# Splitting the first w_out pieces between the merge blocks, and the last output tile in two column halves

## The chip, the cores and the metric

The kernel runs on one core of a Trainium2 chip. The metric is the device time of one execution in microseconds (us); less is better. The core's engines work side by side, each through its own queue of instructions in the order of that queue: TensorE (PE) multiplies into PSUM banks; VectorE (DVE) and ScalarE (ACT) do elementwise work; SyncE (SP) issues most transfers between DRAM and the core's memory (DMA); GpSimd (POOL) does little here. An instruction waits on semaphores for its inputs and for the buffers that it writes.

## The reference

One encoder block on x of 1024 x 1024 in float32. Two mixers, a multi-scale pooling path and a chunked gated linear attention (GLA), are merged by sigmoid gates and projected by w_out; a squared-ReLU MLP and a last norm follow.

```python
def hybrid_mixer(u, w_in, ...):
    z = jnp.einsum('bld,dn->bln', u, w_in)
    a, q, k, v, r, lr, ga, gb = jnp.split(z, IN_SPLITS, axis=-1)
...
    y_a = jnp.einsum('blc,cd->bld', p, w_pool_out)
...
    y_b = jnp.einsum('blc,cd->bld', o.reshape(B, L, GLA_VAL), w_gla_out)
    m = jax.nn.sigmoid(ga) * y_a + jax.nn.sigmoid(gb) * y_b
    return jnp.einsum('bld,de->ble', m, w_out)

def squared_relu_mlp(u, w_ff1, w_ff2):
    hdn = jnp.square(jax.nn.relu(jnp.einsum('bld,df->blf', u, w_ff1)))
    return jnp.einsum('blf,fd->bld', hdn, w_ff2)

def reference(x, meta_tokens, norm_mix, ...):
...
        h = h + hybrid_mixer(rmsnorm(h, norm_mix[l]), ...)
        h = h + squared_relu_mlp(rmsnorm(h, norm_ffn[l]), w_ff1[l], w_ff2[l])
    return rmsnorm(h, norm_final)[:, N_META:]
```

## The kernel before, in words

Every float32 product is made of three matmuls (the helper mm3, lines L280, L281, L282): each operand is split into a high part and a low part, and high x high, high x low and low x high are added in one PSUM bank of 128 x 512. So a weight, once it is loaded, has to be split before PE can use it: ACT copies it to the high part, and DVE subtracts that from the weight for the low part. Bank names in the trace begin with b_: b_mm is a rotating tag, b_oa the last layer's.

The program is written as steps (`step(rest, ...)`) that are recorded in the order of the code and then placed in the engines' queues by a scheduler; an instruction given to `keep_in_program_order` stays where the code has it. Each engine works its queue strictly from front to back, so an instruction that waits holds up everything behind it on its engine.

**The merge stage** (about 479 to 512 us). For the second half of the rows, `yb(j)` (L1316) computes two groups of the merge, d = 2j and 2j + 1, in `yb_block` (L1072): 12 matmuls of the GLA output (tile yg) with w_gla_out into a b_mm bank. The weights of j = 2 and 3 are kept in their split form from before; those of 0 and 1 are loaded again (tile raw) and split into w1h and w1l on ACT L84 and DVE L85, 128 x 1024 at a time. Behind a group DVE multiplies the bank with the gate (L1095, tiles o and t: this frees the bank; the gate gb comes from DRAM by an SP DMA of L1037), adds the other mixer's part (L1096, ma from DRAM), ACT makes the high half th (L1099), and DVE the low half tl (L1100). The projection `out_tile(t, ch)` (L1262) then multiplies a row tile t of the merged result, half by half of the columns ch, with w_out: 24 matmuls, and a DVE add (L1277). `x_again` loads x once more for that add.

w_out's first half arrives in four pieces of 256 rows, kk = 0 to 3, each 128 x 1024 in the core: `load_wo(0, kk)` issues the DMA (L1243), and splits it on ACT (L1244) and DVE (L1245) into the tile wo. Piece kk holds the blocks 2kk and 2kk + 1 of the eight that one out tile adds up, so piece 3 is used by an out tile's last six matmuls. The steps stand in this order: yb(2), the four load_wo, yb(3), yb(0), x_again for rows 0 and 1, out_tile(0, 0), yb(1), out_tile(1, 0), and then the other six.

**The tail** (from about 1209 us). The last of the MLP's second layer's products (`m == 6`) are added for four row tiles, t = 0 to 3, each in a bank b_oa of its own: nine matmuls per row from three late pairs (`product`). Then, row by row: DVE adds the bank to the residual (L1536), `finish_row` squares half a row on ACT with a sum (L1512), computes the inverse root in small steps (L232 to L240), scales half h1 on ACT (L1515) and half h0 on DVE (L1516), and SP issues both output DMAs (L1518).

Of the kernel before, what the change touches and what calls it, by code (L numbers as in the profile page):

```python
# [10 lines left out]
ACT = mybir.ActivationFunctionType  # L11
ALU = mybir.AluOpType
AX = mybir.AxisListType

P = 128
D = 1024
# [3 lines left out]
HALF = 512  # L20
# [9 lines left out]
NPAIR = DFF // P // 2  # L30
# [92 lines left out]
def kernel(  # L123
# [60 lines left out]
    gB = left.push("gB", [P, D], F32)  # L184
# [16 lines left out]
    raw = Raw(nc, [left.push(f"raw{i}", [P, D], F32) for i in range(2)])  # L201
# [10 lines left out]
    def f32(ap):  # L212
        return ap.bitcast(F32)
# [4 lines left out]
    def bcast(v):  # L218
        return v[None, :].broadcast_to([P, D])
# [56 lines left out]
    def mm3(ps, n, lhs, rhs, first=True, last=True, more=False):  # L276

        for i in range(n):
            (ah, al), (bh, bl) = lhs(i), rhs(i)
            pe.matmul(ps, ah, bh, start=first and i == 0, stop=False, skip_group_check=more)  # L280
            pe.matmul(ps, ah, bl, start=False, stop=False, skip_group_check=more)  # L281
            pe.matmul(ps, al, bh, start=False, stop=last and i == n - 1, skip_group_check=more)  # L282
# [83 lines left out]
    def halves():  # L366
        return [slice(h * HALF, (h + 1) * HALF) for h in range(2)]
# [541 lines left out]
    decs = tiny(4 * NC)  # L909
# [75 lines left out]
    rest, fill, done = [], [], set()  # L985
# [80 lines left out]
    def rows4(w, j):  # L1066
        return w[:, j * 256 : (j + 1) * 256].rearrange("(k p) c -> p k c", p=P)
# [143 lines left out]
    MERGE = (2, 3, 0, 1)  # L1211
# [18 lines left out]
    def x_again(*rows):  # L1230
        for t in rows:
            tc.keep_in_program_order(nc.sync.dma_start(S["acc"][:, t], x[t * P : (t + 1) * P, :]))

    def load_wo(ch, kk):
        def fn():
            wo = S["wo"][ch][:, :, 2 * kk : 2 * kk + 2]
            c = slice(ch * HALF, (ch + 1) * HALF)
            src = w_out[kk * 256 : (kk + 1) * 256, c].rearrange("(k p) c -> p k c", p=P)
            if ch:
                r = raw.load(src, D).rearrange("p (k c) -> p k c", k=2)  # L1240
            else:
                r = S["acc"][:, 4 + kk].rearrange("p (k c) -> p k c", k=2)
                nc.sync.dma_start(r, src)  # L1243
            act.activation(wo[:, 0], r, ACT.Copy)  # L1244
            dve.tensor_tensor(wo[:, 1], r, f32(wo[:, 0]), ALU.subtract)  # L1245

        return fn

    step(rest, merge_open)
    def wo1_open():  # L1250
# [77 lines left out]
    step(rest, wo1_open)  # L1328
    for t in range(2, 8):
# [170 lines left out]
    def finish_row(t, tail):  # L1500

        a, (h0, h1) = S["c"][:, t], halves()
        junk = S["w2"]["12"].rearrange("p i c -> p (i c)")[:, (t % 4) * D : (t % 4 + 1) * D]
        if not tail:
            ss = ln_stat[t % 4]
            act.activation(junk, a, ACT.Square, accum_out=ss)
            rs = inv_sqrt(ss, 1, 1.0 / D)
            dve.scalar_tensor_tensor(junk, a, rs, gB, ALU.mult, ALU.mult)
            nc.sync.dma_start(out[t * P : (t + 1) * P, :], junk)
            return  # L1510
        s0, s1 = tails[t]
        act.activation(junk[:, h0], a[:, h0], ACT.Square, accum_out=s0)  # L1512
        dve.tensor_scalar(s1, s1, 1.0 / D, EPS, ALU.mult, ALU.add)
        rs = inv_sqrt(s0, 1, 1.0 / D, s1)
        act.activation(junk[:, h1], a[:, h1], ACT.Copy, scale=rs)  # L1515
        dve.scalar_tensor_tensor(junk[:, h0], a[:, h0], rs, gB[:, h0], ALU.mult, ALU.mult)  # L1516
        for c in (h1, h0):
            nc.sync.dma_start(out[t * P : (t + 1) * P, c], junk[:, c])  # L1518

    tails = [(decs[:, 2 * i : 2 * i + 1], decs[:, 2 * i + 1 : 2 * i + 2]) for i in range(4)]  # L1520

    def ff2():
        nc.sync.dma_start(gB, bcast(norm_final))
        h1 = halves()[1]
        b, late = None, []

        def product(t, i, av, bv):
            (ah, al), (bh, bl) = av, bv
            c = slice(t * P, (t + 1) * P)
            mm3(b[t], 1, lambda _: (ah[:, c], al[:, c]), lambda _: (bh, bl), first=i == 0, last=i == NPAIR - 1)  # L1530

        def leave(m, t, b):
            for r, k, sign in FF2[m][2]:
                a = S["c"][:, 4 * r + t, k * HALF : (k + 1) * HALF]
                if sign > 0:
                    dve.tensor_tensor(a, b[t], a, ALU.add)  # L1536
                else:
                    dve.tensor_tensor(a, a, b[t], ALU.subtract)

        def left_over(m, t, b):  # L1540
            leave(m, t, b)
            if m == 4:
                yield
                finish_row(4 + t, False)
            elif m == 5:
                yield
                a = S["c"][:, t, h1]
                junk = S["w2"]["12"][:, 8 + t]
                act.activation(junk, a, ACT.Square, accum_out=tails[t][1])
                dve.tensor_tensor(a, a, gB[:, h1], ALU.mult)  # L1550
            yield

        def left_overs(m, b):
            for t in range(4):
                yield from left_over(m, t, b)

        todo = iter(())
        for m, i, av, bv in ahead(ff2_operands(), 2):
            if i == 0:
                b = [bank("ob" if m % 2 else "oa") for _ in range(4)]  # L1560
            if m == 6 and i >= NPAIR - 3:
                late.append((i, av, bv))
            else:
                for t in range(4):
                    product(t, i, av, bv)
# [12 lines left out]
    def ff_layers():  # L1578

# [57 lines left out]
```

## Time and profile before

| | |
|---|---|
| median of 3 runs | 1222.71 us (1220.06 to 1222.97) |
| the profiled execution | 1222.77 us, of it 1221.0 us span |
| starts of the last matmul ahead of d7 and of the first of out_tile(1, 0) | 491.04 to 511.76 us |
| longest PE wait in the merge stage | 1.17 us, at 492.59, ended by DVE L1095 |
| PE's last matmul starts | 1212.89 us |
| last output DMA is issued | 1217.6 us |

Times in the trace are counted from the start of the span. A row of the timeline has start, duration, engine, line, operation, output<-input, shapes, and in brackets the idle time of the engine ahead of it and what ended it. SPq is SP's queue of DMA issues; PEld is PE's loading of weights, which runs beside its matmuls. d0 to d7 name the eight groups of the merge; they run in the order 4, 5, 6, 7, 0, 1, 2, 3.

### The profile page before, as it was taken

How to read it: one execution, taken by the hardware profiler on the slowest of the kernel's cores; microseconds unless marked ns; L12 is line 12 of the kernel's file. 1: busy time of each engine (PE TensorE's matmuls, PEld its weight loads, DVE VectorE, ACT ScalarE, POOL GpSimd, SP SyncE). 2: the span in 40 equal slices, each digit the busy share in tenths (PEclk: the TensorE clock that was granted, in tenths of full speed). 3: DMA queues.
4: the chain of work that ended last, by engine and by line, in shares of the span. 5: the costliest groups of instructions: out<-in, count | busy, mean ns of one | idle time of the engine just before them, and what ended most of it. 6: DMA issues, size and time to landing. Idle time of an engine off the chain costs nothing.

```text
span 1221.0 us, 18366 instructions
## 1 busy us (share of the span) xinstructions
PE 1207.9 (99%) x6807; PEld 997.2 (82%) x6807; DVE 838.9 (69%) x1381; ACT 572.0 (47%) x1009; POOL 75.5 (6%) x96
## 2 busy tenths in 40 slices
PE   9999999999999999999999999999999999999997
PEld 6998977778778888788778888888888888888886
DVE  6535657665777569825887677676775887887686
ACT  7627444444456224314655455454554444444544
POOL 0000043222330000000000000000000000000000
PEclk9999999999999999999999999999999999999999
DMA  8313334435247977921244444444569973333532
GB/s 236 93 40 95 118 100 130 147 105 164 81 137 266 318 243 233 323 67 69 104 139 156 141 163 151 150 155 145 172 228 326 332 246 104 96 95 96 171 95 88
DMA packets 153356, 192.76 MB, mean 158 GB/s; under 512 B 12178, under 2 KB 88226, under 8 KB 153267
## 3 DMA queue, kind: packets, MB, share of 16 engines
q1 hardware_dynamic: 153266, 191.59, 48.9%
q8 instruction: 53, 0.87, 0.3%
q14 instruction: 37, 0.30, 0.1%
HBM read 128.62 MB, written 62.93 MB: 157 GB/s over the span
## 4 chain that ended last, share of the span: by engine, by line
PE 89%; DVE 4%; DMA 2%; ACT 2%; issue 2%; POOL 0%; SPq 0%; POOLq 0%; ACTq 0%; DVEq 0%
PE b_mm L280 7%; PE b_mm L282 7%; PE b_mm L281 7%; PE b_y L280 6%; PE b_y L282 6%; PE b_y L281 6%; PE b_oa L282 5%; PE b_oa L281 5%; PE b_oa L280 5%; PE b_z L280 4%; PE b_z L282 4%; PE b_z L281 4%; PE b_sc L280 4%; PE b_ob L281 4%; PE b_ob L282 4%; PE b_ob L280 4%
## 5 line engine op out<-in xcount | busy, mean ns | idle before, releaser
L685 ACT ACTIVATE w1h<-raw 128x512 fp32r<-128x512 f32 x106 | 65.9, 622 | 59.3 <-PE b_y L281 25.3
L686 DVE TENSOR_TENSOR w1l<-raw,w1h 128x512 fp32r<-128x512 f32 x106 | 72.4, 684 | 22.0 <-ACT w1h L685 22.0
L280 PE MATMUL b_sc<-th,w1h 128*128 128x512 f32 x216 | 85.6, 396 | 0.6 <-ACT u2p L1420 0.6
L280 PE MATMUL b_z<-th,w1h 128*128 128x512 f32 x216 | 85.3, 395 | 0.5 <-DVE c L804 0.3
L281 PE MATMUL b_sc<-tl,w1h 128*128 128x512 f32 x216 | 84.9, 393 | 0.0
L281 PE MATMUL b_z<-tl,w1h 128*128 128x512 f32 x216 | 84.3, 390 | 0.4 <-DVE tl L1306 0.4
L282 PE MATMUL b_sc<-th,w1l 128*128 128x512 f32 x216 | 84.4, 391 | 0.0
L685 ACT ACTIVATE w1h<-fs 128x512 fp32r<-128x512 f32 x81 | 51.1, 631 | 70.7 <-PE b_y L281 32.9
L282 PE MATMUL b_z<-th,w1l 128*128 128x512 f32 x216 | 84.1, 389 | 0.0
L686 DVE TENSOR_TENSOR w1l<-fs,w1h 128x512 fp32r<-128x512 f32 x81 | 57.1, 705 | 26.1 <-ACT w1h L685 25.9
L280 PE MATMUL b_mm<-th,w1h 128*128 128x512 f32 (+1 forms) x208 | 72.1, 347 | 0.0
L281 PE MATMUL b_mm<-tl,w1h 128*128 128x512 f32 (+1 forms) x208 | 71.0, 341 | 0.0
L282 PE MATMUL b_mm<-th,w1l 128*128 128x512 f32 (+1 forms) x208 | 71.0, 341 | 0.0
L685 ACT ACTIVATE w1h<-bt 128x512 fp32r<-128x512 f32 x46 | 29.1, 632 | 70.9 <-issue 43.9
L1496 DVE TENSOR_TENSOR bt<-w,w 128x512 f32<-128x512 f32 x80 | 54.6, 683 | 1.0 <-DMA w<-in_w_ff_dram 0.9
L280 PE MATMUL b_mm<-wo,th 128*128 128x512 f32 x128 | 50.4, 393 | 0.0
L282 PE MATMUL b_mm<-wo,tl 128*128 128x512 f32 x128 | 49.9, 390 | 0.0
L281 PE MATMUL b_mm<-wo,th 128*128 128x512 f32 x128 | 49.8, 389 | 0.0
L280 PE MATMUL b_y<-wo,w1h 128*128 128x512 f32 x128 | 49.8, 389 | 0.0
L281 PE MATMUL b_y<-wo,w1h 128*128 128x512 f32 x128 | 49.8, 389 | 0.0
L282 PE MATMUL b_y<-wo,w1l 128*128 128x512 f32 x128 | 49.8, 389 | 0.0
L686 DVE TENSOR_TENSOR w1l<-bt,w1h 128x512 fp32r<-128x512 f32 x46 | 31.7, 690 | 25.6 <-ACT w1h L685 25.6
(405 smaller groups left out, 3334.6 us busy)
## 6 DMA issues: line engine op xcount, KB each, us to landing
hf_dram<-h SPq DMA_DIRECT2D x112, 256.0 KB, 2.1
raw<-hf_dram SPq DMA_DIRECT2D x112, 256.0 KB, 2.6
w<-in_w_ff_dram SPq DMA_DIRECT2D x64, 256.0 KB, 4.5
raw<-in_w_in_dram SPq DMA_DIRECT2D x22, 512.0 KB, 4.3
raw<-in_w_ff_dram SPq DMA_DIRECT2D x16, 512.0 KB, 4.2
rawx<-in_w_ff_dram SPq DMA_DIRECT2D x16, 512.0 KB, 4.2
rawp<-in_w_in_dram SPq DMA_DIRECT2D x10, 512.0 KB, 4.4
xs<-in_x_dram SPq DMA_DIRECT2D x8, 512.0 KB, 4.8
```

The source lines that it names most:

```text
L280: pe.matmul(ps, ah, bh, start=first and i == 0, stop=False, skip_group_check=more)
L281: pe.matmul(ps, ah, bl, start=False, stop=False, skip_group_check=more)
L282: pe.matmul(ps, al, bh, start=False, stop=last and i == n - 1, skip_group_check=more)
L685: act.activation(hi, a, ACT.Copy)
L686: dve.tensor_tensor(lo, a, f32(hi), ALU.subtract)
L1496: dve.tensor_tensor(bt, w, S["w2"][q[3:]][:, i], ALU.add if q[2] == "+" else ALU.subtract)
```

## The change

Two things are rewritten. In the merge stage, all four DMAs of w_out's first half are issued ahead of yb(2) (`fetch_wo`), one piece is split behind each of the four yb blocks (`first_wo`, its two instructions kept in program order), and the out tiles (0, 0) and (1, 0) stand behind all four blocks. In the tail, row 3 is computed by `last_tile` in two column halves of 256: nine matmuls, an add and a square with sum each, the two sums joined by a small add; row 2's scaling and output are put behind row 3's sums; and row 3's two output DMAs are issued by two queues, h1 by ACT's and h0 by SP's.

```diff
+    def split_wo(ch, kk, r):
+        wo = S["wo"][ch][:, :, 2 * kk : 2 * kk + 2]
+        a = act.activation(wo[:, 0], r, ACT.Copy)
+        return a, dve.tensor_tensor(wo[:, 1], r, f32(wo[:, 0]), ALU.subtract)
+
+    def fetch_wo():
+        for kk in range(4):
+            nc.sync.dma_start(wo_place(kk), wo_source(0, kk))
+
+    def first_wo(kk):
+        for ins in split_wo(0, kk, wo_place(kk)):
+            tc.keep_in_program_order(ins)
...
-    yb(2)
-    for k in range(4):
-        step(rest, load_wo(0, k))
-    yb(3)
-    yb(0)
+    step(rest, fetch_wo)
+    for k, j in enumerate(MERGE):
+        yb(j)
+        step(rest, lambda k=k: first_wo(k))
     step(rest, lambda: x_again(0, 1))
     step(rest, out_tile(0, 0))
-    yb(1)
     step(rest, out_tile(1, 0))
...
+        def put():
+            o = act.activation(junk[:, h1], a[:, h1], ACT.Copy, scale=rs)
+            if t > 1:
+                tc.keep_in_program_order(o)
+            (nc.scalar if t == 3 else nc.sync).dma_start(out[t * P : (t + 1) * P, h1], junk[:, h1])
+            dve.scalar_tensor_tensor(junk[:, h0], a[:, h0], rs, gB[:, h0], ALU.mult, ALU.mult)
+            nc.sync.dma_start(out[t * P : (t + 1) * P, h0], junk[:, h0])
+
+        return put
+
+    def last_tile(t, late, product, b, put):
...
+        for q, ss in ((0, decs[:, 8:9]), (1, s0)):
+            c = slice(q * 256, (q + 1) * 256)
+            for x in late:
+                product(t, *x, c)
+            dve.tensor_tensor(a[:, c], b[t][:, c], a[:, c], ALU.add)
+            act.activation(junk[:, c], a[:, c], ACT.Square, accum_out=ss)
+            if q == 0:
+                dve.tensor_tensor(s1, s1, ss, ALU.add)
+        last = finish_tail(t, s0, s1)
+        put()
+        last()
...
-            for t in range(4):
+            for t in range(3):
                 for x in late:
                     product(t, *x)
                 leave(m, t, b)
-                finish_row(t, True)
+                if t < 2:
+                    finish_row(t, True)
+            a, (s0, s1) = S["c"][:, 2], tails[2]
+            act.activation(S["w2"]["12"][:, 4], a[:, : HALF], ACT.Square, accum_out=s0)
+            last_tile(3, late, product, b, finish_tail(2, s0, s1))
```

MERGE is (2, 3, 0, 1). The new lines for what moved: the split is L1242 on ACT and L1243 on DVE, the out tile's add L1284, the half add L1545, the half square L1546, the scalings L1528 and L1532.

First place: DVE's queue in the merge stage, from the last low half of the first half of the rows. Before:

```order
L1245 TENSOR_TENSOR wo0_4699<-acc_4703,wo0_4699 128x1024 [waits DMAHW5_49,Activation_49]
L1100 SCALAR_TENSOR_TENSOR tl0_140<-o_3841,th0_136 128x512 [waits Activation_49]
L1245 TENSOR_TENSOR wo0_4699<-acc_4703,wo0_4699 128x1024 [waits DMAHW6_49,Activation_49]
L1245 TENSOR_TENSOR wo0_4699<-acc_4703,wo0_4699 128x1024 [waits DMAHW7_49,Activation_49]
L85 TENSOR_TENSOR w1l_132<-raw0_120,w1h_128 128x1024 [waits DMAHW1_49,PE_49,Activation_49]
L1095 SCALAR_TENSOR_TENSOR o_4715<-o_4715,b_mm_4780 128x512 [waits DMAHW0_49,PE_49]
L1095 SCALAR_TENSOR_TENSOR t1_4711<-t1_4711,b_mm_4727 128x512 [waits DMAHW5_49,DVE_49]
```

and in the changed kernel, from the same low half (its second row before, its first row now):

```order
L1100 SCALAR_TENSOR_TENSOR tl0_140<-o_3841,th0_136 128x512 [waits Activation_49]
L85 TENSOR_TENSOR w1l_132<-raw0_120,w1h_128 128x1024 [waits DMAHW1_49,PE_49,Activation_49]
L1095 SCALAR_TENSOR_TENSOR t1_4711<-t1_4711,b_mm_4731 128x512 [waits DMAHW3_49,DVE_49]
L1095 SCALAR_TENSOR_TENSOR o_4715<-o_4715,b_mm_4774 128x512 [waits DMAHW0_49,PE_49]
L1096 TENSOR_TENSOR t1_4711<-t1_4711 128x512 [waits DMAHW4_49,DVE_49]
L1095 SCALAR_TENSOR_TENSOR t1_4711<-t1_4711,b_mm_4750 128x512 [waits DMAHW5_49]
L1096 TENSOR_TENSOR o_4715<-o_4715 128x512 [waits DMAHW1_49,DVE_49]
L1100 SCALAR_TENSOR_TENSOR tl1_148<-t1_4711,th1_144 128x512 [waits Activation_49]
```

Three splits of w_out have left the place between that low half and the first merge instructions. The last of the four now stands here, behind the low half of the last group (d3, whose bank is b_mm_4871):

```order
L1243 TENSOR_TENSOR wo0_4699<-acc_4703,wo0_4699 128x1024 [waits Activation_49]
L1100 SCALAR_TENSOR_TENSOR tl1_148<-o_4715,th1_144 128x512 [waits Activation_49]
L1095 SCALAR_TENSOR_TENSOR o_4715<-o_4715,b_mm_4871 128x512 [waits DMAHW3_49,PE_49]
L1096 TENSOR_TENSOR o_4715<-o_4715 128x512 [waits DMAHW1_49,DVE_49]
L1100 SCALAR_TENSOR_TENSOR tl1_148<-o_4715,th1_144 128x512 [waits Activation_49]
L1243 TENSOR_TENSOR wo0_4699<-acc_4703,wo0_4699 128x1024 [waits Activation_49]
```

From the first merge instruction L1095 to this last split, 28 rows stand on DVE: L85 once, L1243 three times, and 24 rows of 128x512.

Second place: PE's queue in out_tile(0, 0), from its 13th matmul to its 21st. Before, where yb(1) still stands behind it:

```order
L280 MATMUL b_mm_4859<-wo0_4699,th0_136 128x512
L281 MATMUL b_mm_4859<-wo0_4699,th0_136 128x512
L282 MATMUL b_mm_4859<-wo0_4699,tl0_140 128x512
L280 MATMUL b_mm_4859<-wo0_4699,th0_136 128x512
L281 MATMUL b_mm_4859<-wo0_4699,th0_136 128x512
L282 MATMUL b_mm_4859<-wo0_4699,tl0_140 128x512
L280 MATMUL b_mm_4859<-wo0_4699,th0_136 128x512 [waits Activation_49]
L281 MATMUL b_mm_4859<-wo0_4699,th0_136 128x512
```

and now, behind yb(1):

```order
L280 MATMUL b_mm_4893<-wo0_4699,th0_136 128x512 [waits Activation_49]
L281 MATMUL b_mm_4893<-wo0_4699,th0_136 128x512 [waits DVE_49]
L282 MATMUL b_mm_4893<-wo0_4699,tl0_140 128x512
L280 MATMUL b_mm_4893<-wo0_4699,th0_136 128x512
L281 MATMUL b_mm_4893<-wo0_4699,th0_136 128x512
L282 MATMUL b_mm_4893<-wo0_4699,tl0_140 128x512
L280 MATMUL b_mm_4893<-wo0_4699,th0_136 128x512 [waits Activation_49]
L281 MATMUL b_mm_4893<-wo0_4699,th0_136 128x512 [waits DVE_49]
```

Each of the pieces 2, 3 and 4 (kk = 1, 2, 3) is now waited for where it is first used, its high half by L280 for ACT and its low half by L281 for DVE; the rows shown are those of the third and the fourth piece.

Third place: PE's last matmuls, row 3 of the tail, where the first column half ends and the second begins. Before, the row's nine matmuls are 512 wide and none of them waits. Now:

```order
L280 MATMUL b_oa_9704<-w1h_128 128x256
L281 MATMUL b_oa_9704<-w1l_132,w1h_128 128x256
L282 MATMUL b_oa_9704<-w1h_128,w1l_132 128x256
L280 MATMUL b_oa_9704<-fxh_7802,w1h_128 128x256 [waits DVE_49]
L281 MATMUL b_oa_9704<-fxl_7806,w1h_128 128x256
```

The first matmul of the second half carries a wait for DVE; both halves write the same bank, b_oa_9704.

More of the change, by code (lines that the diff above doesn't have):

```diff
@@ L1232, in x_again, with wo_source, wo_place @@
             tc.keep_in_program_order(nc.sync.dma_start(S["acc"][:, t], x[t * P : (t + 1) * P, :]))
-    def load_wo(ch, kk):
[L1235 to L1247, printed above, removed]
+    def wo_source(ch, kk):
+        return w_out[kk * 256 : (kk + 1) * 256, ch * HALF : (ch + 1) * HALF].rearrange("(k p) c -> p k c", p=P)
+    def wo_place(kk):
+        return S["acc"][:, 4 + kk].rearrange("p (k c) -> p k c", k=2)
+    def split_wo(ch, kk, r):
[8 more added lines that the diff above has]
+            tc.keep_in_program_order(ins)
+    def load_wo(ch, kk):
+        return lambda: split_wo(ch, kk, raw.load(wo_source(ch, kk), D).rearrange("p (k c) -> p k c", k=2)) and None
     step(rest, merge_open)
@@ L1512, in finish_row, with finish_tail @@
         act.activation(junk[:, h0], a[:, h0], ACT.Square, accum_out=s0)
+        finish_tail(t, s0, s1)()
+    def finish_tail(t, s0, s1):
+        a, (h0, h1) = S["c"][:, t], halves()
+        junk = S["w2"]["12"].rearrange("p i c -> p (i c)")[:, t * D : (t + 1) * D]
         dve.tensor_scalar(s1, s1, 1.0 / D, EPS, ALU.mult, ALU.add)
         rs = inv_sqrt(s0, 1, 1.0 / D, s1)
[L1515 to L1518, printed above, removed]
+        def put():
[7 more added lines that the diff above has]
+    def last_tile(t, late, product, b, put):
+        a, (s0, s1) = S["c"][:, t], tails[t]
+        junk = S["w2"]["12"].rearrange("p i c -> p (i c)")[:, t * D : (t + 1) * D]
+        for q, ss in ((0, decs[:, 8:9]), (1, s0)):
[9 more added lines that the diff above has]
+        last()
     tails = [(decs[:, 2 * i : 2 * i + 1], decs[:, 2 * i + 1 : 2 * i + 2]) for i in range(4)]
@@ L1525, in ff2, with product @@
         b, late = None, []
-        def product(t, i, av, bv):
+        def product(t, i, av, bv, w=slice(0, HALF), stop=False):
             (ah, al), (bh, bl) = av, bv
             c = slice(t * P, (t + 1) * P)
-            mm3(b[t], 1, lambda _: (ah[:, c], al[:, c]), lambda _: (bh, bl), first=i == 0, last=i == NPAIR - 1)
+            mm3(
+                b[t][:, w], 1, lambda _: (ah[:, c], al[:, c]), lambda _: (bh[:, w], bl[:, w]),
+                first=i == 0, last=i == NPAIR - 1 or (stop and i == NPAIR - 4), more=w.stop - w.start < HALF,
+            )
         def leave(m, t, b):
@@ L1564, in ff2 @@
                 for t in range(4):
-                    product(t, i, av, bv)
+                    product(t, i, av, bv, stop=m == 6 and t == 3)
                 next(todo, None)
```

## The prediction

> **What bounds the kernel now.** I read the page's busy shares and its chain first.
>
> ```profile
> span 1221.0 us, 18366 instructions
> PE 1207.9 (99%) x6807; PEld 997.2 (82%) x6807; DVE 838.9 (69%) x1381; ACT 572.0 (47%) x1009; POOL 75.5 (6%) x96
> ...
> PE 89%; DVE 4%; DMA 2%; ACT 2%; issue 2%; POOL 0%; SPq 0%; POOLq 0%; ACTq 0%; DVEq 0%
> ```
>
> TensorE (PE) is busy for 99% of the span and holds 89% of the chain that ends last. The number of multiplied columns does not change, so an edit can win only where PE stands idle, or behind PE's last matmul. The list of PE's waits says how much that is.
>
> ```profile
> PE b_ms L449 <- POOL xr L445: 1.5, 1, 1.5
> PE b_mm L280 <- DVE o L1095: 1.2, 1, 1.2
> ```
>
> Columns: total us, times, longest. The second row is the one wait in the stretch that the change touches. The chain, and the timelines of PE and of VectorE (DVE) there, tell where it comes from.
>
> ```profile
> 480.07 5.53 DMA acc<-in_w_out_dram
> ...
> 485.61 1.07 ACT wo L1244
> ...
> 490.72 1.22 DVE w1l L85
> ```
>
> ```profile
> 488.45 2.35 DVE L1245 TENSOR_TENSOR wo<-acc,wo 128x1024 fp32r<-128x1024 f32 x2
> ...
> 491.86 0.68 DVE L1095 SCALAR_TENSOR_TENSOR o<-o,b_mm 128x512 f32<-128x512 f32 x1
> 492.46 0.68 DVE L1095 SCALAR_TENSOR_TENSOR t<-t,b_mm 128x512 f32<-128x512 f32 x1
> ...
> 497.80 1.22 DVE L85 TENSOR_TENSOR w1l<-raw,w1h 128x1024 fp32r<-128x1024 f32 x1
> 498.94 0.68 DVE L1100 SCALAR_TENSOR_TENSOR tl<-t,th 128x512 fp32r<-128x512 f32 x1
> ```
>
> ```profile
> 488.09 0.39 PE L281 MATMUL b_mm<-yg,w1h 128*128 128x512 f32 x1
> ...
> 491.04 0.39 PE L282 MATMUL b_mm<-yg,w1l 128*128 128x512 f32 x1
> 492.59 0.50 PE L280 MATMUL b_mm<-yg,w1h 128*128 128x512 f32 x1 [1.17 <-DVE o L1095]
> ...
> 511.76 0.39 PE L280 MATMUL b_mm<-wo,th 128*128 128x512 f32 x1
> ```
>
> Call the eight merge groups d4, d5 (from yb(2)), d6, d7 (yb(3)), d0, d1 (yb(0)), d2, d3 (yb(1)): 12 matmuls each, in this order. DVE does the low halves of the w_out pieces (L1245) and a weight split (L85) first; only then comes the merge's first instruction L1095 at 491.86, which frees PE's bank, and d7 starts at 492.59. Matmuls stand 0.227 us apart, so d7 was due at 491.04 + 0.23 = 491.27. From there to the start of out_tile(1,0) at 511.76 lie 84 matmuls, 84 x 0.2267 = 19.04 us: 20.49 - 19.04 = 1.45 us were lost. **That is all the merge half of the change can win**, 0.12% of the time.
>
> **The merge stage, part by part.** Counts do not change there: the same matmuls, four w_out DMAs, four splits. What changes is the place of the splits on DVE and ScalarE (ACT), and that both out tiles stand behind d3 on PE.
>
> *What it removes.* On DVE the weight split L85 is now the first work after d4's last instruction. It needs ACT's half L84, which needs the matmul at 488.09.
>
> ```profile
> 489.00 1.05 ACT L84 ACTIVATE w1h<-raw 128x1024 fp32r<-128x1024 f32 x1
> ```
>
> A matmul's result is out 0.43 us after its start (1212.89 and 1213.32 in the last fence), so L84 can start at 488.52 (it waited for wo work until 489.00) and end at 489.57; L85 runs from 489.60. A 128x1024 DVE step moves the next on by 1.14 us (497.80, 498.94), a 128x512 one by 0.60 (491.86, 492.46). So the first merge add stands at 490.74, ends at 491.42, and d7 starts at about 491.45. **The stall shrinks from 1.45 to about 0.3 us** (0.18, and 0.11 for a first matmul of 0.50 instead of 0.39): -1.15.
>
> *What it adds.* DVE had nothing to do from 487.2 to 489.6, where before it did splits; that time is gone, and the splits now stand behind merges. Between the add at 490.74 and the split of piece 4 the order has 28 DVE rows: L85 and three w_out pieces at 1.14, and 24 of 128x512 at 0.60. That is 4.56 + 14.40 = 18.96, so 509.70 without a wait. Waits known from the rows: a dependent pair is 0.72 apart and not 0.60 (+0.11); d3's tl waits for ACT's 0.63 (+0.77); ACT's half of piece 4, 1.05 long, stands behind that (+0.36); three more, worked out in the same way, make 0.57: d6's result is out at 491.04 + 0.43 = 491.47 (0.13), L84 of the next split stands behind a matmul of d7 (0.27), and one tl behind an ACT th (0.17).
>
> ```profile
> 480.89 0.63 ACT L1099 ACTIVATE th<-t 128x512 fp32r<-128x512 f32 x1 [3.27 <-DVE t L1096]
> ```
>
> ```profile
> 511.97 0.69 DVE L1095 SCALAR_TENSOR_TENSOR o<-o,b_mm 128x512 f32<-128x512 f32 x1
> 512.69 0.69 DVE L1096 TENSOR_TENSOR o<-o 128x512 f32<-128x512 f32 x1
> ```
>
> The last wait is d1's gate, a load from DRAM, and here the trace gives no single price:
>
> ```profile
> 505.06 0.69 DVE L1095 SCALAR_TENSOR_TENSOR t<-t,b_mm 128x512 f32<-128x512 f32 x1 [1.52 <-DMA t<-gb_dram]
> ...
> 499.64 0.32 SPq L1037 DMA_DIRECT2D t<-gb_dram  x1
> ```
>
> ```profile
> t<-gb_dram SPq DMA_DIRECT2D x2, 256.0 KB, 3.5
> ```
>
> It was issued at 499.64 and used at 505.06, 5.4 us later; behind 48 matmuls' worth of out_tile(0,0) and d2 nobody saw it. The median of two such gates from 495 to 506 is 3.5. Now it is issued when the tl that frees its buffer ends, about 497.2, and DVE reaches it at 501.2. At 3.5 us it lands at 500.7 and costs nothing; at 5.4 it costs 1.4. So the split of piece 4 starts at 490.74 + 18.96 + 1.81 = 511.5 (gate on time) to 512.9 (as late as before), and its low half is there 1.25 later, at **512.8 to 514.2**.
>
> *When PE wants it.* PE does d7, d0 to d3 without out_tile between: 60 matmuls from 491.56 (with the 0.11), 13.60 us, so out_tile(0,0) starts at about 505.16. Its piece 4 is used from the 19th matmul (high half, waits for ACT) and the 20th (low half, waits for DVE): 509.24 and 509.47. The high half is there at 511.5 to 512.9, the low one as above. **PE stands still there for about 3.3 to 4.7 us** counted to the start of the 20th matmul, and 0.11 more for that restart. The spare 5.4 us that out_tile(0,0) gave the merges, between d1 and d2, is what is given up. Sum: 0.3 + 3.3 + 0.1 - 1.45 = +2.3 at the one end, 0.3 + 4.7 + 0.1 - 1.45 = +3.7 at the other. The second is the row of the same gate, the first the median of its kind; I take +3.1, between them, a little nearer to the same gate. Behind it PE remains the bound, so nothing gives the time back: d2's and d3's adds are late too, but two out tiles lie behind.
>
> Edits at nothing: the four w_out loads are issued from 479.1 in both, 512 KB each in some 5.5 us (the chain's row), and land 7 us or more before the first split at 497.7; if that cover were gone, a piece's DMA time would stand in front of its split. x_again's loads stay behind d1 and are used only by adds behind an out tile; SP issues each in about 0.4 us. If they came late, the adds wait, not PE, as long as a bank is free.
>
> **The tail.** Durations for half the width, and the end before:
>
> ```profile
> 60.68 0.28 PE L280 MATMUL b_mm<-vw,th 128*128 128x256 f32 x1
> ...
> 60.80 0.28 PE L281 MATMUL b_mm<-vw,th 128*128 128x256 f32 x1
> ```
>
> ```profile
> L956 DVE TENSOR_TENSOR gi<-n,ends 128x256 f32<-128x256 f32 x8 | 3.0, 415 | 0.0
> ```
>
> ```profile
> L409 ACT ACTIVATE vo<-b_mm 128x256 f32<-128x256 f32 x16 | 6.2, 385 | 20.5 <-PE b_mm L282 11.2 <-DVE lrtok L404 9.3
> ```
>
> ```profile
> 1211.08 0.39 PE L280 MATMUL b_oa<-fxh,w1h 128*128 128x512 f32 x1
> ...
> 1212.89 0.39 PE L282 MATMUL b_oa<-w1h,w1l 128*128 128x512 f32 x1
> 1213.32 0.69 DVE L1536 TENSOR_TENSOR c<-b_oa,c 128x512 f32<-128x512 f32 x1
> ...
> 1214.04 0.63 ACT L1512 ACTIVATE w<-c 128x512 f32<-128x512 f32 x1 [0.28 <-DVE c L1536]
> 1214.55 0.75 DVE L1516 SCALAR_TENSOR_TENSOR w<-c,small,gB 128x512 f32<-128x512 f32 x1
> ...
> 1216.46 0.72 ACT L1515 ACTIVATE w<-c,small 128x512 f32<-128x512 f32 x1 [0.67 <-DVE small L240]
> 1216.47 0.75 DVE L1516 SCALAR_TENSOR_TENSOR w<-c,small,gB 128x512 f32<-128x512 f32 x1
> ```
>
> ```profile
> L1518 SPq DMA_DIRECT2D out_dram<-w x8: 332/358/432, 1211.1 to 1217.6; - x8
> ...
> DMA to landing us min/median/max: 2.0/2.1/2.3
> ```
>
> The first half's nine matmuls run from 1211.08 at 0.12 each, result at about 1212.4; DVE's half add (0.42) ends at 1212.9. Both halves lie in one bank, and the first matmul of the second half carries a wait for DVE in the order: it starts at about 1212.93 instead of 1212.16, 0.8 late, and its result comes at 1214.35, against 1213.32 before. The half add and half square give back 0.27 + 0.25, and ACT's square is ready about 0.5 later than before. Behind it stands row 2's scaled write (0.75) on DVE, ahead of row 3's small steps, so the last scaling starts at about 1216.8, 0.35 late. The second queue returns that: the last DMA was issued at 1217.6 behind one of 0.36 us (1217.2); now each half has its own queue, and SP's goes out at 1217.6 again. **Tail: 0**, from -0.4 (the halves overlap) to +0.8: no row shows a DMA issued by ACT; at SP's 0.36 it costs nothing, at twice that 0.4 more.
>
> [...]
>
> **The sum.** The profiled execution took 1222.77 us (span 1221.0 and 1.8 around it), the median is 1222.71. 1222.77 + 3.1 + 0 = **1225.9**. 0.3%, about what a measurement of this kernel can tell from no change, is 3.7 us: faster means below 1219.0, slower above 1226.4.
>
> **Rivals.**
>
> *A, the stall goes and nothing follows* (the other side, below before): 1222.8 - 1.15 - 0.4 = 1221.2. It decides at piece 4: if its low half is there by 509.47, nothing stalls. For it: DVE is busy only 69% over the whole span. Against it: the count of 28 rows alone, without one wait, puts the low half at 509.70 + 1.25 = 510.95, 1.5 us late. 0.07.
>
> *B, half of it:* the waits on top of the 28 rows overlap, piece 4 at about 511: 511.0 - 509.2 + 0.1 - 1.45 = +0.5, 1223.3. It decides by whether ACT's halves are ready when DVE comes; against it stands d3's chain of add, th, tl, which no order shortens. 0.15.
>
> *C, gates late everywhere:* d4's gate is issued once the tl that stood at 487.85 is done; that tl now starts at about 486.5, so about 487.2, and the gate is needed at 490.74, 3.5 later. At 5.4 it lands at 492.6: the first stall stays as it was, and all merges behind it shift by up to 1.9, d1's late gate with them. The low half of piece 4 then comes at about 516, against 491.27 + 79 x 0.2267 = 509.18 for an undisturbed PE: 6.9 + 0.1 - 1.45 = +5.5 in all, 1228.3, slower. For it: the row at 505.06, and the DMA share of 0.87 to 0.95 in these windows.
>
> ```profile
> 496.00:500.00 4.00, 4.00 (x20) 3.30 (x19) 4.00 (x7) 1.69 (x3) 0.00 (x0) 1.00 0.87 313
> 500.00:504.00 4.00, 4.00 (x19) 3.34 (x18) 3.40 (x6) 1.23 (x2) 0.00 (x0) 1.00 0.95 316
> ```
>
> (PE, PEld, DVE, ACT, POOL, clock, DMA share, GB/s.) Against it:
>
> ```profile
> 488.56 0.32 SPq L1037 DMA_DIRECT2D t<-gb_dram  x1
> ```
>
> This is d4's gate before; its add ran at 492.46 without a wait, 3.9 us later, so that here at least 3.9 was enough. 0.20.
>
> **How the numbers follow.** Forecast (+2.3 to +3.7, and the tail's -0.4 to +0.8) 0.58, A 0.07, B 0.15, C 0.20. Faster by over 0.3% takes more than all that is lost there: 0.03, kept for what I have not seen. Slower: C but for a part, and the upper edge of the forecast: 0.33. Within: 0.64. The range leaves out half of A and half of C: 1222.0 to 1227.7.
>
> **What would show it.** In the profile after: d7's first matmul at about 491.5; the PE wait of 1.2 on L1095 gone or below 0.3; new PE waits in out_tile(0,0), on ACT's and DVE's pieces, of together about 3.3 to 4.7 us; DVE without idle time from 490.7 to the last split; a PE wait of about 0.8 on DVE within the last row. Wrong would be: no PE wait in out_tile(0,0) (A), a d7 that still starts at 492.6 (C), or time that goes anywhere else than these two places.

## The result, and the profile after

| | before | changed |
|---|---|---|
| median, runs of the first comparison | 1222.94 us (1220.06 to 1223.54, 6 runs) | 1227.67 us (1225.33 to 1230.06, 6 runs) |
| ratio | | 1.0048, 95% interval 1.0035 to 1.0060 |
| profiled execution, its span | 1222.77, 1221.0 us | 1225.33, 1223.5 us |

The changed kernel is slower by 0.48%, 0.0048 x 1222.9 = 5.9 us by the ratio and 4.7 us by the medians. The prediction's time was 1225.9 us with a range of 1222.0 to 1227.7, and it put most of its chance (0.64) on a difference within 0.3%. The time lies at the range's upper end, and the difference is clear of 0.3%.

The two spans must not be subtracted as they stand. The start of the kernel, which the change does not touch, took 2.45 us less in this execution than in that of before; both starts occur in other kernels here too (the second low half of vw stands at 17.75 to 18.06 us in seven of the traces and at 20.33 to 20.66 in six others; before's 26 runs of a later comparison form one group at 1219.97 to 1220.82 and one at 1222.45 to 1223.62). Two landmarks on VectorE take it out: the second low half of vw at the start, and the fourth out tile's add behind the merge stage. Timeline of before, DVE:

```profile
20.43 1.23 DVE L382 TENSOR_TENSOR vw<-raw,vw 128x1024 fp32r<-128x1024 f32 x1
...
533.72 0.69 DVE L1277 TENSOR_TENSOR acc<-b_mm,acc 128x512 f32<-128x512 f32 x1 [2.08 <-PE b_mm L282]
```

and of the changed kernel:

```profile
17.98 1.22 DVE L382 TENSOR_TENSOR vw<-raw,vw 128x1024 fp32r<-128x1024 f32 x1 [0.32 <-ACT vw L381]
...
535.93 0.69 DVE L1284 TENSOR_TENSOR acc<-b_mm,acc 128x512 f32<-128x512 f32 x1 [4.75 <-PE b_mm L282]
```

From the one to the other it is 533.72 - 20.43 = 513.29 us before and 535.93 - 17.98 = 517.95 now: **the merge stage became 4.66 us longer.** The tail is measured against row 3's first matmul: the span ended 1221.0 - 1211.08 = 9.9 us behind it before, and 1223.5 - 1213.30 = 10.2 now, about +0.3. Together about +5 us.

Where the 4.66 us are, the list of PE's waits in the stage shows first (total, times, longest):

```profile
PE b_mm L280 <- ACT wo L1242: 2.1, 1, 2.1
PE b_mm L281 <- DVE wo L1243: 1.0, 2, 0.8
PE b_mm L280 <- DVE t L1095: 0.2, 1, 0.2
```

The wait of 1.2 on L1095 has become one of 0.2, and the late pieces cost 2.1 + 1.0. That is 3.3 against 1.2, a difference of 2.1; it does not explain 4.66. Piece 4 comes late from DVE's queue, 21.4 us from the first merge instruction to its split:

```profile
488.40 0.69 DVE L1095 SCALAR_TENSOR_TENSOR t<-t,b_mm 128x512 f32<-128x512 f32 x1
...
509.83 1.23 DVE L1243 TENSOR_TENSOR wo<-acc,wo 128x1024 fp32r<-128x1024 f32 x1 [0.25 <-ACT wo L1242]
```

PE's timeline has the rest, in the matmuls behind the waits:

```profile
507.35 0.40 PE L282 MATMUL b_mm<-wo,tl 128*128 128x512 f32 x1
509.85 0.50 PE L280 MATMUL b_mm<-wo,th 128*128 128x512 f32 x1 [2.10 <-ACT wo L1242]
511.11 0.79 PE L281 MATMUL b_mm<-wo,th 128*128 128x512 f32 x1 [0.76 <-DVE wo L1243]
511.69 0.63 PE L282 MATMUL b_mm<-wo,tl 128*128 128x512 f32 x1
512.12 0.63 PE L280 MATMUL b_mm<-wo,th 128*128 128x512 f32 x1
...
514.25 0.55 PE L282 MATMUL b_mm<-wo,tl 128*128 128x512 f32 x1
514.63 0.40 PE L280 MATMUL b_mm<-wo,th 128*128 128x512 f32 x1
```

Matmuls of 128x512 take 0.63 us there instead of 0.39 and start 0.43 apart instead of 0.227. The windows of the stage (us, PE, PEld, DVE, ACT, POOL, granted clock, DMA share, GB/s) name the cause:

```profile
507.00:509.00 2.00, 0.75 (x4) 0.26 (x2) 1.27 (x3) 0.78 (x2) 0.00 (x0) 1.00 1.02 331
509.00:511.00 2.00, 0.50 (x1) 0.19 (x1) 1.75 (x3) 2.00 (x3) 0.00 (x0) 1.00 1.02 408
511.00:513.00 2.00, 1.89 (x5) 1.51 (x6) 2.00 (x3) 1.64 (x2) 0.00 (x0) 0.54 0.94 373
513.00:515.00 2.00, 2.00 (x7) 1.61 (x6) 1.69 (x3) 0.00 (x0) 0.00 (x0) 0.61 0.68 242
515.00:517.00 2.00, 2.00 (x11) 1.64 (x10) 0.46 (x1) 0.00 (x0) 0.00 (x0) 1.00 0.87 252
```

The granted clock fell to half for some 3.4 us after PE had stood still. From 511.11 to 514.63 PE did eight steps in 3.52 us; at the steps measured with the clock at 1.00, 0.34 for the first behind a wait and 0.227 for seven, they take 1.93. So 1.6 us of the stage's 4.66 are slow matmuls. In all PE loses 6.1 us between 480 and 540 against a step of 0.227 per matmul, where it lost 1.45 before: again 4.66 more.

### The profile page after: what moved, and what is told of

It reads as the page before. It is cut to its first block, busy times and chain, and to the rows that moved or that the text cites. A ratio compares the mean times of both kernels' runs of the same rounds, so it can differ in the third digit from the quotient of the medians.

```text
span 1223.5 us, 18388 instructions
## 1 busy us (share of the span) xinstructions
PE 1207.5 (99%) x6816; PEld 997.5 (82%) x6816; DVE 838.9 (69%) x1383; ACT 571.6 (47%) x1011; POOL 75.7 (6%) x96
## 4 chain that ended last, share of the span: by engine, by line
PE 91%; DVE 4%; DMA 3%; issue 1%; ACT 1%; POOL 0%; SPq 0%; DVEq 0%; ACTq 0%; POOLq 0%
PE b_mm L280 7%; PE b_mm L282 7%; PE b_mm L281 7%; PE b_y L280 6%; PE b_y L281 6%; PE b_y L282 6%; PE b_oa L280 5%; PE b_oa L282 5%; PE b_oa L281 5%; PE b_z L280 4%; PE b_z L281 4%; PE b_z L282 4%; PE b_sc L280 4%; PE b_ob L280 4%; PE b_ob L282 4%; PE b_ob L281 4%
## 5 line engine op out<-in xcount | busy, mean ns | idle before, releaser
L280 PE MATMUL b_sc<-th,w1h 128*128 128x512 f32 x216 | 85.6, 396 | 0.7 <-ACT u2p L1425 0.7
L280 PE MATMUL b_z<-th,w1h 128*128 128x512 f32 x216 | 85.2, 395 | 0.5 <-DVE c L804 0.4
L281 PE MATMUL b_sc<-tl,w1h 128*128 128x512 f32 x216 | 84.9, 393 | 0.0
L281 PE MATMUL b_z<-tl,w1h 128*128 128x512 f32 x216 | 84.3, 390 | 0.4 <-DVE tl L1313 0.4
L280 PE MATMUL b_mm<-th,w1h 128*128 128x512 f32 (+1 forms) x208 | 72.1, 347 | 0.0
L281 PE MATMUL b_mm<-tl,w1h 128*128 128x512 f32 (+1 forms) x208 | 71.0, 342 | 0.0
L280 PE MATMUL b_mm<-wo,th 128*128 128x512 f32 x128 | 51.0, 398 | 2.1 <-ACT wo L1242 2.1
L281 PE MATMUL b_mm<-wo,th 128*128 128x512 f32 x128 | 50.8, 397 | 1.0 <-DVE wo L1243 1.0
L281 PE MATMUL b_y<-wo,w1h 128*128 128x512 f32 x128 | 49.8, 389 | 0.0
L280 PE MATMUL b_y<-wo,w1h 128*128 128x512 f32 x128 | 49.8, 389 | 0.0
```

## The experiments

In the expectations, M is the theory that the merge half holds the loss, "place" the theory that what counts is where the splits stand on DVE, and "clock" the theory that PE's idle time lowers its clock. "PE loses" means the time by which the steps between PE's matmuls in the stage exceed 0.227 us, as above.

**The two halves apart.** The first kernel, the merge half alone, has the changed merge stage and before's tail; the second, the tail half alone, is the reverse.

> The merge half of the change, with the tail of before. Theory M (the merge stage holds the whole loss: the stall of 1.2 at d7 goes, pieces of w_out come late on DVE, and the stall they make also drops PE's granted clock to 0.5 for some 3 us): the stage is 4.5 us longer than before's, the time about 1227.3; PE waits 2.1 and 0.8 in out_tile(0,0), and windows with a clock of 0.5 behind them. Rival T (a good part of the loss is the tail): the stage 2 to 3 us longer, the time at most 1225.5.

Measured: 1228.77 us beside 1222.52, ratio 1.0059 (1.0045 to 1.0073). PE lost 8.0 us, 6.6 more than in before; 2 more than in the changed kernel, whose merge stage is the same program. The waits of 2.1 and 0.8 and the half clock are there; in addition d7 waited 1.0 and piece 3 1.0, since gates landed later in this execution. Its windows show the drop, and that it lasts about 3.4 us (columns as above):

```profile
512.00:514.00 2.00, 1.24 (x4) 0.82 (x5) 2.00 (x2) 1.46 (x2) 0.00 (x0) 0.90 1.01 412
514.00:516.00 2.00, 2.00 (x6) 1.52 (x5) 1.81 (x3) 1.27 (x2) 0.00 (x0) 0.50 1.02 401
516.00:518.00 2.00, 2.00 (x8) 1.58 (x8) 1.31 (x2) 0.00 (x0) 0.00 (x0) 0.75 0.81 265
```

> The tail half of the change, with the merge stage of before. Theory M: within 0.5 us of before (the wait of 0.6 of the second column half and row 2's late scaling are given back by the second queue); from row 3's first matmul to the last issue of an output DMA 6.5 us as in before. Rival T: 1.5 us or more slower.

Measured: 1223.19 us, ratio 1.0006 (0.9995 to 1.0018); the last output DMA was issued at 1220.17, 6.54 us behind row 3's first matmul at 1213.63. M holds: the loss is in the merge half. This execution also showed that before's merge stage itself can fall into the slow clock: d7 waited longer than in the profile of before, and its matmuls went to 0.63.

```profile
493.16 0.50 PE L280 MATMUL b_mm<-yg,w1h 128*128 128x512 f32 x1 [1.86 <-DVE o L1095]
...
494.50 0.63 PE L282 MATMUL b_mm<-yg,w1l 128*128 128x512 f32 x1
```

It lost 3.8 us in the stage where the profile of before lost 1.45.

**The clock.** The merge half, with matmuls of no use that write a spare bank while PE would wait for piece 4. Their result is read by nothing. `FILL` is (9, 4).

```diff
+                def fill(n):
+                    for _ in range(n):
+                        pe.matmul(spare, MH[0][:, 0, at : at + P], wo[:, 0, 0], start=True, stop=True)
...
+                    if k == 6:
+                        fill(FILL[0])
                     pe.matmul(b, ah, bh, start=k == 0, stop=False)
+                    if k == 6:
+                        fill(FILL[1])
                     pe.matmul(b, ah, bl, start=False, stop=False)
```

> The merge half, and in out_tile(0,0) 13 matmuls of no use into a spare bank, 9 ahead of the wait for piece 4's high half and 4 ahead of its low half, so that PE has no long idle time there. Theory clock (PE's idle time drops its clock, which costs 1.6 us behind the stall): the waits of 2.1 and 0.8 become work, the clock stays at 1.00, and the stage is 1.3 to 1.7 us shorter than that of the merge half alone, although PE does 13 matmuls more. Rival (the slow matmuls have another cause, such as the DMA traffic or the splits of the second half of w_out beside them): clock and matmul times as in the merge half alone, the stage equal or up to 0.4 us longer.

Measured: 1225.08 us, ratio 1.0032 (1.0020 to 1.0045), where the merge half alone had 1.0059 in the same comparison. The clock stayed at 1.00:

```profile
509.00:511.00 2.00, 1.95 (x9) 1.32 (x8) 1.04 (x3) 1.93 (x3) 0.00 (x0) 1.00 0.96 346
511.00:513.00 2.00, 2.00 (x9) 1.43 (x9) 2.00 (x3) 2.00 (x3) 0.00 (x0) 1.00 1.03 420
513.00:515.00 2.00, 2.00 (x10) 1.65 (x9) 2.00 (x4) 0.50 (x1) 0.00 (x0) 1.00 0.90 334
```

DVE's splits and a DMA share near 1 stand beside these matmuls as in the changed kernel, so neither made matmuls slow there. PE lost 2.5 us and did 13 x 0.227 = 2.9 us of filling, 5.5 together against 8.0. That is 2.5 less, where 1.3 to 1.7 was expected: 1.6 are slow matmuls that are gone (in the merge half alone the ten steps from 513.08 to 517.05 took 3.97 us instead of 0.34 + 9 x 0.227 = 2.38), and the other 0.9 goes with gates that landed at other times. The theory of the clock holds: thirteen useless matmuls made this kernel faster than the merge half alone. It is not only the profiled execution: the mean granted clock of a whole execution was 0.996 to 0.997 in all five of the merge half and 0.995 to 0.996 in all six of the changed kernel, but 0.998 to 0.999 in all nine with the filling and in before's 26.

Two variants ask how much idle time it takes: `FILL` of (0, 4), then of (5, 0).

> The merge half with only the four matmuls of no use between piece 4's high and low half; the wait of 2.1 ahead of it stays. Theory clock, with an idle time between 1.3 and 1.9 us as the limit: the wait of 2.1 alone drops the clock to 0.5 for about 3.3 us. Rival (it takes both waits, 2.9 us in all): the clock stays at 1.00.

> The merge half with five matmuls of no use ahead of the wait for piece 4's high half, so that about 1.0 of the 2.1 us is left, then the wait of 0.8 for the low half. Theory clock: no single idle time above 1.3, the clock stays at 1.00 (or drops only if the sum of the two, 1.8, is what counts). Rival (the slow matmuls follow the splits of the second half of w_out): clock of 0.5 as in the merge half alone.

Measured: one run each, 1229.15 and 1228.93 us. With the second gap alone filled, the single wait of 2.10 was enough: the clock was 0.59 and 0.56 in the two windows from 515 to 519. With half of the first gap filled the waits were 0.97 and 0.76, and the clock stayed at 1.00 from 511 to 521; but this execution had a d7 that waited 2.19, and there the clock fell to 0.50:

```profile
494.00:496.00 2.00, 2.00 (x7) 1.59 (x8) 2.00 (x4) 0.63 (x1) 0.00 (x0) 0.71 0.67 256
496.00:498.00 2.00, 2.00 (x6) 1.51 (x6) 1.40 (x3) 0.00 (x0) 0.00 (x0) 0.50 0.75 206
498.00:500.00 2.00, 2.00 (x10) 1.65 (x9) 0.77 (x1) 1.86 (x3) 0.00 (x0) 0.94 0.91 332
```

So the clock fell behind waits of 1.86, 2.10 and 2.19 us, and not behind single waits of 1.0, 1.17 and 1.60 (the next kernel's).

The length of one wait does not tell when the clock fell, though. All five drops last 3.40 to 3.41 us. In the changed kernel the clock's record of 1.00 begins at 5.97 us; the clock falls at 511.15, rises at 514.56 and falls for good at 1217.70: 148, 1 and 206 times 3.413 us from one to the next. In before it begins at 13.23 and falls for good at 1218.14, 353 times 3.413. In these two traces, then, the changes lie on a grid of 3.413 us, and not at the same times in both. Windows of that length follow, for the merge half alone and the tail half set by their drops at 513.61 and 494.37, and for the next kernel (columns as above):

```profile
506.78:510.19 3.41, 1.93 (x6) 1.04 (x6) 3.35 (x5) 0.63 (x1) 0.00 (x0) 1.00 0.90 311
510.19:513.61 3.42, 1.03 (x3) 0.67 (x4) 2.50 (x3) 2.87 (x4) 0.00 (x0) 1.00 0.99 380
513.61:517.02 3.41, 3.41 (x9) 2.64 (x8) 3.22 (x4) 1.66 (x2) 0.00 (x0) 0.50 0.93 362
```

```profile
490.96:494.37 3.41, 1.55 (x7) 1.02 (x6) 3.41 (x5) 1.06 (x1) 0.00 (x0) 1.00 0.91 292
494.37:497.78 3.41, 3.41 (x10) 2.62 (x9) 3.41 (x6) 1.11 (x2) 0.00 (x0) 0.50 0.75 247
```

```profile
488.96:492.37 3.41, 2.83 (x13) 2.02 (x11) 3.32 (x3) 2.49 (x3) 0.00 (x0) 1.00 1.02 363
492.37:495.78 3.41, 2.39 (x10) 1.99 (x11) 3.13 (x5) 0.62 (x1) 0.00 (x0) 1.00 0.92 324
```

PE's idle time is the first column less the second. In the merge half alone it was 1.48 us in one window, and the next one kept its clock; it was 2.39 in that one, and the next ran at half. In the tail half it was 1.86, and the next ran at half. The wait of 1.60 us in the next kernel lies across a boundary of its windows, 0.58 on one side and 1.02 on the other, so it does not tell what 1.60 in one window would do. Up to the tail the clock fell in five of the 14 traces (their mean granted clock is 0.996 to 0.997, that of the other nine 0.998 to 0.999). The window of 3.41 us ahead of the drop held idle time of 1.86 us in the tail half, 2.08 in the variant (0, 4), 2.19 in the variant (5, 0), 2.39 in the merge half alone and 2.86 in the changed kernel; no drop follows a window with 1.48 or less. What lies between was not met up to the tail, and no run placed a wait against the grid on purpose, so a limit on the length of a single wait, between 1.60 and 1.86 us, would fit these drops as well.

**The place of the splits.** The out tiles behind all four blocks as in the change, but the four splits behind yb(2) as before; the tail is that of before. The difference from the changed kernel in the merge stage:

```diff
     step(rest, fetch_wo)
-    for k, j in enumerate(MERGE):
-        yb(j)
-        step(rest, lambda k=k: first_wo(k))
+    yb(2)
+    for k in range(4):
+        step(rest, lambda k=k: split_wo(0, k, wo_place(k)) and None)
+    yb(3)
+    yb(0)
+    yb(1)
```

> The out tiles behind all four merge blocks as in the change, but the four w_out pieces split behind yb(2) as before, in the order that the scheduler gives them; tail of before. Theory place (the loss is where the splits stand on DVE, not that the out tiles wait behind yb(1)): PE waits at d7 as before (1.2 to 1.9) and nowhere in out_tile(0,0); PE loses 1.4 to 2.2 us in the stage (before: 1.45), with up to 2 more where that wait drops the clock; time 1222 to 1224. Rival out (moving yb(1) ahead takes away the 5.4 us that hid the gates): new waits of 1 us and more in d2, d3 or the first out tiles, 3 us and more lost.

Measured: 1220.83 us beside 1221.33, ratio 0.9998 (0.9988 to 1.0009). PE lost 1.9 us, all at d7:

```profile
PE b_mm L280 <- DVE t L1095: 1.6, 1, 1.6
```

Nothing waits in d2, d3 or the out tiles. So moving yb(1) ahead is free by itself; the loss comes from the splits behind the merges, the last of which is then wanted before DVE reaches it.

**Giving the late pieces time.** Still the changed splits, with before's tail, but the first two out tiles share the wait: first 18 matmuls of each and then six of each, or piece by piece.

```diff
+        for k0, k1 in ((0, 4), (4, 6), (6, 8)):
+            for t in range(2):
+                w = slice(t * P, (t + 1) * P)
+                mm3(
+                    b[t], k1 - k0, lambda i: (MH[0][:, k0 + i, w], ML[0][:, k0 + i, w]),
+                    lambda i: (wo[:, 0, k0 + i], wo[:, 1, k0 + i]), first=k0 == 0, last=k1 == 8,
+                )
```

(The 18-matmul form has `((0, 6), (6, 8))`.)

> The merge half, with the first two out tiles interleaved: the first 18 matmuls of out_tile(0,0), the first 18 of out_tile(1,0), then the last six of each; the DVE order is that of the merge half. Theory M: piece 4 is now wanted 18 matmuls (4.1 us) later than before, and its stall of 2.1 + 0.8 us goes with the clock drop; what is left is 0.3 at d7 and 0.3 at piece 3. The stage is 0.7 to 1.1 us shorter than before's, the time about 1222.0. Rival (DVE is late for everything behind, so a new wait comes at the next bank or the next tile): the stage 1 us or more longer than before's.

> The merge half, with the first two out tiles interleaved piece by piece: 12 matmuls of each, then 6 of each twice; DVE's order is that of the merge half; tail of before. Theory place: the third piece is now wanted 24 matmuls (5.4 us) and the fourth 36 (8.2 us) behind the start, later than both come; what is left is 0.3 to 1.1 at d7. PE loses 0.3 to 1.2 us in the stage (before 1.45, the 18-matmul form 2.3), no clock below 1.00 there; time 0.3 to 1.1 us below before's. Rival (late gates put DVE so far back that something else waits): 2 us or more lost, the time of before or slower.

Measured: 1.0009 (0.9999 to 1.0019) and 1.0007 (0.9999 to 1.0016). Both took the long wait and the clock drop away and so brought the time back to before's, but neither reached the gain. The 18-matmul form lost 2.3 us, most of it at piece 3 (waits of 0.2 on ACT and 1.0 on DVE); the other lost 1.7, more than the 0.3 to 1.2 expected, of it 1.0 at d7. DVE's timeline of the second shows what stands there now:

```profile
489.52 1.23 DVE L85 TENSOR_TENSOR w1l<-raw,w1h 128x1024 fp32r<-128x1024 f32 x1 [2.41 <-ACT w1h L84]
491.41 0.69 DVE L1095 SCALAR_TENSOR_TENSOR t<-t,b_mm 128x512 f32<-128x512 f32 x1 [0.67 <-DMA t<-gb_dram]
```

DVE is free and waits 0.67 us for d4's gate. In the 18-matmul form d1's gate kept DVE waiting for 1.64 us; behind it DVE has hardly any idle time up to the split of piece 3, which came late with it:

```profile
500.80 0.69 DVE L1095 SCALAR_TENSOR_TENSOR t<-t,b_mm 128x512 f32<-128x512 f32 x1 [1.64 <-DMA t<-gb_dram]
...
506.34 1.22 DVE L1243 TENSOR_TENSOR wo<-acc,wo 128x1024 fp32r<-128x1024 f32 x1
```

**A version meant to beat both.** Two pieces split in DVE's idle time ahead of yb(2), the third behind yb(3), the fourth behind yb(0), the out tiles piece by piece, and the tail with two banks (below).

> A version meant to be better than both: the first two w_out pieces split ahead of yb(2), where DVE and ACT stand idle for more than two us in the change, the third behind yb(3), the fourth behind yb(0); the first two out tiles behind all four blocks and interleaved piece by piece; the tail with two banks. Theory place: d7 waits about 0.5 and nothing else, PE loses 0.5 to 1.1 in the stage instead of 1.45, the tail ends 0.4 earlier: 0.8 to 1.4 us below before. Rival (the gates from DRAM, not the splits, set the merges' pace): 1.5 us or more lost in the stage, the time within 0.5 of before.

Measured: 1222.20 us, ratio 1.0007 (0.9997 to 1.0016), no difference. PE lost 1.2 us, a single wait of 0.9 at d7, and again DVE waited for d4's gate:

```profile
487.42 1.22 DVE L85 TENSOR_TENSOR w1l<-raw,w1h 128x1024 fp32r<-128x1024 f32 x1
489.09 0.69 DVE L1095 SCALAR_TENSOR_TENSOR t<-t,b_mm 128x512 f32<-128x512 f32 x1 [0.45 <-DMA t<-gb_dram]
490.34 0.69 DVE L1095 SCALAR_TENSOR_TENSOR t<-t,b_mm 128x512 f32<-128x512 f32 x1 [0.56 <-DMA t<-gb_dram]
```

**The tail.** Before's merge stage, and the changed tail with both last DMAs on SP; then with a bank of its own for the second half's late matmuls (`own = bank("ob")`, and one more add of 128x256 ahead for what the first bank holds).

> The tail half alone with both output DMAs of the last row issued by SP. Theory (the second queue saves SP's issue of one DMA): from row 3's first matmul to the issue of the last output DMA 6.9 us instead of 6.5, and the end of the span 0.2 to 0.4 us later against that matmul. Rival (the second queue saves nothing, its issue on ACT is as late): equal within 0.1.

> The tail half alone, the second column half's late matmuls in a bank of its own (what the first bank holds of it is added before, by one more DVE add of 128x256 and beside PE's work). Theory bank (the wait of 0.6 comes from DVE reading the bank that PE wants to write): no PE wait between the halves, row 3's last matmul 0.7 to 0.9 us earlier against its first, and the last output DMA's issue 0.3 to 0.6 earlier against it (6.0 instead of 6.5). Rival (row 2's work on DVE and ACT sets the end, not PE): the last matmul earlier, but the last issue within 0.2 of 6.5.

Measured, one run each, 1220.80 and 1220.04 us. With one queue the last issue came 1215.61 - 1208.70 = 6.91 us behind row 3's first matmul, as expected, but the span still ended 1218.9 - 1208.70 = 10.2 behind it, as with two queues and not the 0.2 to 0.4 later that was expected: the second queue issues earlier and ends nothing earlier. The DMA view from 1217 us on of the changed kernel (KB each, median us to landing) shows where it goes:

```profile
out_dram<-w SPq DMA_DIRECT2D x3, 256.0 KB, 2.2
out_dram<-w ACTq DMA_DIRECT2D x1, 256.0 KB, 2.7
```

The DMA issued by ACT lands after 2.7 us, those of SP after 2.2 (the landing of SP's last one is not in the trace). From the last issue to the end of the span it is 1223.5 - 1219.82 = 3.7 us with two queues and 1218.9 - 1215.61 = 3.3 with one, so what the issue gained is lost behind it. In both kernels the last transfers move some 350 to 410 GB/s; that the two at once share this rate is an estimate from these figures, and no run separates it from the queue.

In the changed kernel PE waits between the halves:

```profile
1215.09 0.38 PE L280 MATMUL b_oa<-fxh,w1h 128*128 128x256 f32 x1 [0.56 <-DVE c L1545]
```

With two banks no matmul waits there; the row's last matmul starts 2.03 us behind its first (2.84 in the changed kernel, 1.81 before), the last issue is 5.68 behind that first matmul and the span ends 9.5 behind it, 0.4 earlier than before:

```profile
1209.65 0.28 PE L282 MATMUL b_oa<-w1h,w1l 128*128 128x256 f32 x1
1209.77 0.28 PE L280 MATMUL b_ob<-fxh,w1h 128*128 128x256 f32 x1
```

> The kernel with before's merge stage and the tail in two banks once more, timed: its last output DMA was issued 5.68 us after row 3's first matmul (before 6.5) and its span ended 9.5 after it (before 9.9). If that is the whole difference, the time is 0.3 to 0.5 us below before's; if something earlier pays for the additional DVE step, it is equal or above.

Measured: 1222.79 us beside 1220.78, ratio 1.0007 (0.9998 to 1.0017). Its trace again ends 9.5 us behind row 3's first matmul, but the timing doesn't show the 0.4 us: it is a sixth of the 2.5 us by which starts differ. Whether it is a gain of the whole program stays open.

## Why the prediction was right or wrong

- **The gain at d7** was right in its mechanism and size: d7 started 0.3 us late, as worked out, and its wait on L1095 is 0.2. That gates could take its place (rival C's first half) also came true in other executions of the same merge code: 1.0 us in the merge half alone and 2.2 in the variant (5, 0).
- **The late pieces** were right: PE waits in out_tile(0,0), on ACT for piece 4's high half and on DVE for its low half. Predicted were 3.3 to 4.7 us, all at piece 4; measured were 3.3 there and 0.5 at piece 3, where no wait was predicted, about 3.8 together. The order of 28 rows at 0.60 and 1.14 carried that: from the first merge instruction to the split of piece 4 it was 21.4 us, against 511.5 - 490.74 = 20.8 to 512.9 - 490.74 = 22.2 predicted.
- **The sum is where it failed.** The step reads "PE stands still there for about 3.3 to 4.7 us" and then adds that, a restart of 0.11 and the gain at d7 to +3.1. It prices a wait of PE at its own length. Waits of together 2.9 us also cost half the clock of 3.4 us behind them: 1.6 us in the changed kernel and 1.6 in the merge half alone. The prediction has no such term, although its wait of 2.3 to 3.7 us for piece 4's high half (511.5 to 512.9 against 509.24) is longer than the single waits of 1.86 to 2.19 us behind which the runs show the drop. With that term the forecast would have been 3.1 + 1.6 = +4.7, beyond 0.3%, and the stage measured +4.66; that the two agree so closely is in part luck, since +3.1 holds a stall of about 4.1 where 3.8 was measured. The page of before could not show it at a glance: its only PE wait of the stage was 1.17, and all its windows there have a clock of 1.00.
- **The tail** was right in its steps: PE waits 0.56 between the halves, the last scaling starts 5.75 us behind row 3's first matmul against 5.39 (predicted 0.35 late), the last issue is at 6.5 as before. The end is about 0.3 later all the same, since the price "the second queue returns that" was counted to the issue and not to the landing.
- **The wait between the halves**, priced at 0.8 us from the one bank and the wait in the order, was right: with two banks the row's last matmul starts 2.03 us behind its first instead of 2.84. What PE and DVE in one bank at the same time would do is not shown, since no run here lets them.
- **Rivals A and B** fell: the low half of piece 4 was there at 509.83 + 1.23 = 511.06, on the scale of before (2.45 later) at 513.5, where A wants 509.47 and B about 511. Where the out tiles shared the wait piece by piece and no late piece stalled PE for long, d7 still waited 0.9 us, with DVE waiting for d4's gate ahead of it.

## What to carry to other kernels

Before work is moved from the time in which an engine idles to a place behind other work on that engine, count its rows up to the one that is wanted, and set the sum against the moment of the want: an engine with 69% on the page can have next to no room in the stage (DVE was busy for 19.6 of the 21.4 us up to the split of piece 4). Price a long wait of PE at more than its length: here 1.6 us on top, where PE stood idle for 1.86 us or more of one window of 3.41. Where it can't be avoided, break it up: other tiles' matmuls between (ratios of 1.0007 and 1.0009 to before, where the merge half alone had 1.0059), or even useless ones (1.0032). When two executions are compared, take the stage between two landmarks, not the spans.

## What the runs showed of the hardware that was not expected

- Ahead of the tail PE's granted clock fell to 0.50 for 3.40 to 3.41 us in five traces, each time behind a window of 3.41 us in which PE idled 1.86 us or more, and stayed at 1.00 behind windows with 1.48 or less; in the changed kernel and in before its changes lie on a grid of 3.413 us. The drop set in well behind the restart in the tail half (restart at 493.16, half clock from 494.37). In the kernel with the splits in their old place a wait of 1.60 us lay as 0.58 and 1.02 in two windows, without a drop.
- The same merge program lost 6.1 us in one execution and 8.0 in another, with gates that landed at different times; a loss that follows DRAM loads needs more than one profile.
- With the last two output DMAs of 256 KB issued at the same time by two queues, ACT's landed after 2.7 us, against 2.0 to 2.3 for SP's in the kernel before, and the span ended 3.7 us behind the last issue instead of 3.3: a second queue brought nothing at the end of this program.
